# One decoder layer on one core: the score maxima of heads 2 to 4 moved ahead of the attention, and a higher rate for the recurrences

## The chip, the core and the metric

The kernel runs on one core of a Trainium2 chip. The metric is device time in microseconds (us) for one execution. TensorE (PE in the profile; its weight loads are PEld) does the matmuls, VectorE (DVE) the elementwise work and reductions, ScalarE (ACT) the activations and copies, GpSimd (POOL) some elementwise work; SyncE (SP), ACT and POOL issue the DMAs. Each engine takes its own instructions strictly in the order of the program, and semaphores tie them together. An instruction at the head of a queue that waits holds all that stands behind it on that engine.

## The reference

One layer of a hybrid decoder for 1024 prompt tokens and 8 single-token decode streams. One input projection of the residual is split among four head groups: a gated delta rule (A), RWKV-7 mixing (B), forgetting attention (C) and causal pooling (D). Each gives 512 columns, which are gated with a SiLU and go through one output projection and a layer norm. What the change touches is group C for the prompt, a causal attention of 8 heads of 64 with a decay in the scores:

```python
def _fox_block(qb, cqb, qpos, k, v, ck, kpos):
    s = jnp.einsum('nqhd,nshd->nhqs', qb, k) * (HEAD_DIM ** -0.5)
    s = s + jnp.swapaxes(cqb, 1, 2)[..., :, None] - jnp.swapaxes(ck, 1, 2)[..., None, :]
    s = jnp.where((kpos[None, :] <= qpos[:, None])[None, None], s, NEG_INF)
    return jnp.einsum('nhqs,nshd->nqhd', jax.nn.softmax(s, axis=-1), v)
```

The decode streams attend in the same way to 4096 cached tokens each, whose keys and values lie in pages in HBM.

## The kernel before, in words

The input projection comes as 57 column tiles of 128. A tile (`project`, line 343 on) is 144 matmuls: 16 slices of the depth, three groups of 344 token columns, and three products of split operands (lines 308 to 310). The last 24 tiles (`inputs_cd`) are the queries, the pooling inputs and gates, then keys, values and gates of group C.

Beside the tiles run *fillers*: Python generators that emit a piece of other work at each step. `fill` is called four times for each tile and adds a filler's rate to its account; the filler takes steps until the account is used up. In `inputs_cd` there are two: the cached attention's key side, and `recurrent` with the rate RATE_R. `recurrent` goes through the two recurrences (`chain_b`, `chain_a`), the pooling, the normalisation of group B, and last `c_first`, which starts on group C. What a generator has left when the tiles are done is emitted by `drain`, after the last tile. The emitted program is then put in an order by a scheduler, so that emission is a priority and not yet the order; but `anchored` ties what `c_first` issues to after the last projection matmul emitted so far (`self.last`).

The softmax of a head subtracts the exact row maximum. `c_max` makes it: for each of 8 blocks of 128 queries one or two matmuls of the queries and keys (tiles `cqm`, `ckx`, line 785, up to 512 columns), a mask (line 788), and a row maximum over them on DVE (tile `cmx`, line 789): 12 score tiles for a head. Then the 8 maxima are joined (`cm`, line 792), transposed on PE (line 794), negated by ACT (`cmt`, line 796) and split (`cmh`, `cml`). `c_scores` prepares a head: `c_load` brings queries and keys with four DMAs (`cqr`, `ckr`; lines 763 to 766) and copies them on ACT (`cqm` line 767, `ckx` line 769); the head's operands `cqq` (ACT, line 823), `cqx` (DVE, line 824) and `ckk` (POOL, lines 825 and 826) follow, then the maxima, which two small DMAs bring into the rows `cmr` (line 831) and DVE into `cqx` (line 832). `cqr` and `ckr` have one buffer each for all heads, so that the next head's `ckr` load waits until POOL has read this head's.

A head listed in EARLY has its maxima made ahead: `c_first` loads it, makes the maxima and keeps `cmh` and `cml`. Its `c_scores` later loads queries and keys once more, but leaves out the maxima. All the early heads share one `cqm` and one `ckx` buffer with head 0. Their score tiles (name `a`) have two PSUM buffers.

Then `branch_c` does the attention, head by head, 12 score tiles `s` for each, with `c_scores` of the head after next as a filler at rate 1.1 and the value side of the cached attention (`decode_v`, tile `dkv`) at 0.7. `c_attend` for a score tile: two matmuls (`s`, lines 849 and 850) and a mask, exp on ACT (`cpt`), a rounding copy on ACT (`cph`), a subtraction on DVE (`cpl`, line 861), and three value matmuls (`v`, lines 868 to 870). At the end of each half of a head DVE copies the numerator (`cnum`, line 873). The output projection (`o`) follows.

Of the kernel before, what the change touches and what calls it, by code (L numbers as in the profile page):

```python
# [17 lines left out]
N = T + NS  # L18
G3 = 344
GROUPS = (392, 384, 256)  # L20
RATE_R = 1.0
EARLY = (1,)
RATE_P = 1
SPOOL = {0: 99, 1: 99, 2: 0}
NPOOL = {392: 8, 384: 10, 256: 8}
# [154 lines left out]
class Kernel:  # L180
# [591 lines left out]
    def c_max(self, KX, QM, keep=""):  # L772

        nc = self.nc
        one = self.cp[0]
        mx = self.t(one, [128, 8, 2], "cmx", bufs=2)
        nc.gpsimd.memset(mx, NEG)
        for qi in range(8):
            for b in range((qi + 4) // 4):
                k0, k1 = 512 * b, min(512 * b + 512, 128 * qi + 128)  # L780
                n = k1 - k0
                w = max(n, 256)
                ps = self.ps(self.ctag())
                last = k1 == 128 * qi + 128
                nc.tensor.matmul(ps[:, :w], lhsT=QM[:, qi * 128:qi * 128 + 128], rhs=KX[0:66, k0:k0 + w],
                                 start=True, stop=not last)
                if last:
                    nc.tensor.matmul(ps[:, n - 128:n], lhsT=self.identb, rhs=self.mq, start=False, stop=True)
                nc.vector.reduce_max(mx[:, qi, b:b + 1], ps[:, :n], axis=AX.X)
            yield 1  # L790
        m8 = self.t(one, [128, 8], "cm8", bufs=2)
        nc.vector.tensor_tensor(m8, mx[:, :, 0], mx[:, :, 1], op=ALU.max)
        ps = self.ps(self.ctag())
        nc.tensor.transpose(ps[0:8, 0:128], m8, self.ident)
        mt = self.t(one, [8, 128], "cmt", bufs=1)
        nc.scalar.activation(mt, ps[0:8, 0:128], AF.Copy, scale=-1.0)
        mh, ml = (self.t(one, [8, 128], f"{x}{keep}", F32R, bufs=1) for x in ("cmh", "cml"))
        nc.vector.tensor_copy(mh, mt)
        nc.vector.tensor_tensor(ml, mt, mh.bitcast(F32), op=ALU.subtract)
        return mh, ml  # L800

    def c_first(self, pool):

        for h in EARLY:
            _, _, KX, QM = self.c_load(h, pool)
# [1077 lines left out]
    def inputs_cd(self, sp):  # L1883
# [3 lines left out]
        self.add(self.cached(), RATE_L)  # L1887
        self.add(self.recurrent(**R), RATE_R)
        for t in self.seq[33:]:
# [77 lines left out]
```

## Time and profile before

| | |
|---|---|
| median of 3 timed runs | 2399.89 us (2399.39 to 2400.68) |
| the profiled execution | 2396.94 us, of which the span of instructions is 2395.2 us |
| busy: PE, PEld, DVE, ACT, POOL | 2282.6, 2023.0, 1364.7, 938.4, 295.0 us |
| mean granted TensorE clock | 0.979 of full speed |
| last projection matmul starts | 1717.16 us after the span's start |
| attention of the 8 heads | 1717.3 to 1920.6 us |

A PE that is busy in the profile is not PE at its peak, since the ends of its pipelined matmuls are modelled. The stretch that matters here is the border between the last projection tile and the first heads of the attention; the rows of it stand below.

### The profile page before, as it was taken

To read this page: it belongs to the slowest core of one execution; us is meant where nothing else is said; L and a number is where in the kernel's file an instruction comes from. 1 tells how busy PE (TensorE), PEld (TensorE's weight loads), DVE (VectorE), ACT (ScalarE), POOL (GpSimd) and SP (SyncE) were. 2 spreads that over 40 slices of the span, in tenths; PEclk is the share of its full clock that TensorE was granted. 3 is DMA by queue.
4 is the path that set the end of the run, shared out by engine and by line. 5 is a ranking of instruction groups with operands and counts; after the bars stand their busy time and mean duration, and the time that the engine had idled before them with its cause. 6 is when DMAs were issued, how large, how long until landed. Compare 5 with 4: busy or idle time off the path is not lost. (4 is left out here: it accounts for less than half of the span.)

```text
span 2395.2 us, 47251 instructions
## 1 busy us (share of the span) xinstructions
PE 2282.6 (95%) x17640; PEld 2023.0 (84%) x17640; DVE 1364.7 (57%) x2676; ACT 938.4 (39%) x1853; POOL 295.0 (12%) x408
## 2 busy tenths in 40 slices
PE   8999999999899999999999999999899999999984
PEld 8999999998899999787787877899755578889984
DVE  4665757677576557432222245555578644564598
ACT  5644445434454444121111122454366665211244
POOL 0000000000000000103111121100132110100175
PEclk9999999999999999999999999999999999999997
DMA  6133323545523336778878888653488775683212
GB/s 215 56 100 95 104 85 95 151 106 120 113 81 94 89 107 142 172 187 264 274 250 283 259 273 288 232 161 107 124 260 248 223 282 192 219 304 129 88 63 88
DMA packets 369664, 402.44 MB, mean 168 GB/s; under 512 B 204877, under 2 KB 228350, under 8 KB 368666
## 3 DMA queue, kind: packets, MB, share of 16 engines
q1 hardware_dynamic: 307698, 263.83, 37.3%
q10 hardware_dynamic: 50056, 101.60, 13.9%
q0 software_dynamic: 11680, 33.99, 4.3%
q8 instruction: 139, 2.28, 0.4%
q14 instruction: 91, 0.75, 0.1%
HBM read 314.56 MB, written 84.67 MB: 167 GB/s over the span
## 5 line engine op out<-in xcount | busy, mean ns | idle before, releaser
L308 PE MATMUL pj<-xh,wlo 128*128 128x344 f32 x2688 | 873.1, 326 | 16.7 <-DVE wlo L303 8.6
L309 PE MATMUL pj<-xl,whi 128*128 128x344 f32 x2688 | 871.5, 324 | 0.0
L310 PE MATMUL pj<-xh,whi 128*128 128x344 f32 x2688 | 865.2, 324 | 0.0
L308 PEld LDWEIGHTS pj<-xh,wlo 128*128 128x128 f32 x2688 | 508.1, 189 | 37.1 <-issue 11.4
L309 PEld LDWEIGHTS pj<-xl,whi 128*128 128x128 f32 x2688 | 508.5, 189 | 19.8 <-issue 14.4
L310 PEld LDWEIGHTS pj<-xh,whi 128*128 128x128 f32 x2688 | 507.9, 189 | 16.4 <-issue 13.1
L302 ACT CAST whi<-raw 128x256 fp32r<-128x256 f32 (+1 forms) x504 | 213.0, 424 | 732.6 <-PE pj L310 530.2
L303 DVE TENSOR_TENSOR wlo<-raw,whi 128x256 fp32r<-128x256 f32 (+1 forms) x504 | 226.8, 452 | 365.5 <-ACT whi L302 356.1
L309 PE MATMUL o<-gl,whi 128*128 128x344 f32 x576 | 185.8, 323 | 0.0
L308 PE MATMUL o<-gh,wlo 128*128 128x344 f32 x576 | 184.6, 325 | 0.8 <-ACT gh L1695 0.5
L310 PE MATMUL o<-gh,whi 128*128 128x344 f32 x576 | 185.1, 321 | 0.0
L308 PEld LDWEIGHTS o<-gh,wlo 128*128 128x128 f32 x576 | 107.9, 188 | 21.8 <-DVE y L1720 9.4
L309 PEld LDWEIGHTS o<-gl,whi 128*128 128x128 f32 x576 | 109.0, 189 | 2.3 <-DVE ps L1221 0.9
L310 PEld LDWEIGHTS o<-gh,whi 128*128 128x128 f32 x576 | 109.0, 189 | 0.8 <-issue 0.8
L365 ACT ACTIVATE stg<-pj 128x344 f32<-128x344 f32 x168 | 74.6, 457 | 74.2 <-PE pj L310 73.0
L997 PE MATMUL k<-dkv,dqb 128*32 128x256 f32 x1024 | 88.4, 394 | 15.1 <-DMA dkv<-in_ck 9.0
L1720 DVE TENSOR_TENSOR y<-y,o 128x344 f32<-128x344 f32 x96 | 48.0, 510 | 57.3 <-PE o L310 57.0
L1105 PE MATMUL k<-dkv,dpT 128*8 128x512 f32 x512 | 71.5, 635 | 0.8 <-DMA dkv<-in_cv 0.8
L861 DVE TENSOR_TENSOR cpl<-cpt,cph 128x512 fp32r<-128x512 f32 (+1 forms) x96 | 60.9, 653 | 15.7 <-ACT cph L860 14.9
L308 PE MATMUL o<-gh,wkl 128*128 128x392 f32 (+2 forms) x192 | 63.9, 333 | 0.6 <-DVE wkl L303 0.5
L310 PE MATMUL o<-gh,wkh 128*128 128x392 f32 (+2 forms) x192 | 63.6, 331 | 0.0
L309 PE MATMUL o<-gl,wkh 128*128 128x392 f32 (+2 forms) x192 | 63.3, 330 | 0.0
(597 smaller groups left out, 3321.9 us busy)
## 6 DMA issues: line engine op xcount, KB each, us to landing
dkv<-in_ck SPq DMA_DIRECT2D x256, 256.0 KB
dkv<-in_cv SPq DMA_DIRECT2D x256, 256.0 KB
raw<-in_w ACTq DMA_DIRECT2D x228, 256.0 KB
out_pj<-stg ACTq DMA_DIRECT2D x33, 516.0 KB
bop<-bop SPq DMA_DIRECT2D x16, 1024.0 KB
raw<-in_wo ACTq DMA_DIRECT2D x64, 256.0 KB
aop<-aop SPq DMA_DIRECT2D x16, 768.0 KB
aop<-aost SPq DMA_DIRECT2D x40, 256.0 KB
```

What stands on the lines that cost most here:

```text
L302: nc.scalar.copy(hi, raw)
L303: nc.vector.tensor_tensor(lo, raw, hi.bitcast(F32), op=ALU.subtract)
L308: nc.tensor.matmul(ps, lhsT=wlo, rhs=xh, start=start, stop=False)
L309: nc.tensor.matmul(ps, lhsT=whi, rhs=xl, start=False, stop=False)
L310: self.last = nc.tensor.matmul(ps, lhsT=whi, rhs=xh, start=False, stop=stop).ins
L365: self.nc.scalar.activation(dst[:, g * G3:g * G3 + G3], ps[g], func)
L861: nc.vector.tensor_tensor(pl[:, off:], pt[:, off:], ph[:, off:].bitcast(F32), op=ALU.subtract)
L997: nc.tensor.matmul(ps[32 * hp:32 * hp + 32], lhsT=qb[:, hp, b], rhs=kt[:, :, hp], start=b == 0, stop=b == 7)
L1105: mm = lambda i: nc.tensor.matmul(po[32 * i:32 * i + 8], lhsT=pTv[:, c, :, 4 * bg + i], rhs=t[i // 2][:, i % 2], start=False, stop=c == 31)
L1720: nc.vector.tensor_tensor(y[:, s], y[:, s], ps[g], op=ALU.add)
```

## The change

The list EARLY goes from head 1 to heads 1 to 4, RATE_R from 1.0 to 1.3, and `c_max` gives way to the other fillers after every second block of queries instead of after each.

```diff
-RATE_R = 1.0
-EARLY = (1,)
+RATE_R = 1.3
+EARLY = 1, 2, 3, 4
...
                 nc.vector.reduce_max(mx[:, qi, b:b + 1], ps[:, :n], axis=AX.X)
-            yield 1
+            if qi % 2:
+                yield 1
```

In the order of instructions nothing changes on any engine for the first 7948 rows of PE, with both recurrences in them. From there on the normalisation of group B (tile names `py`, `pz`) and all of group C stand otherwise. One line more in the file moves line numbers above 789 up by one.

The first place is PE where the projection ends. Before, the matmul after the last projection tile (`pj`) is the first score tile of head 0's attention (`s`); the maxima of heads 1 and 0 stand earlier, among the projection's matmuls:

```order
L308 MATMUL pj_20934<-xh_28_130,wlo_21042 128x344
L309 MATMUL pj_20934<-xl_44_146,whi_21041 128x344
L310 MATMUL pj_20934<-xh_28_130,whi_21041 128x344
L849 MATMUL s_21174<-cqq_20424,ckk_20423 128x512
L850 MATMUL s_21174<-cqx_20425,ckx_20414 128x512
```

Now the maxima of heads 1, 2 and 3 stand among the projection's matmuls, and behind the last of these come head 3's transposed maxima (`cm_2727`) and then the score tiles `a` of head 4 (`ckx_20381`):

```order
L309 MATMUL pj_21151<-xl_44_146,whi_21242 128x344
L310 MATMUL pj_21151<-xh_28_130,whi_21242 128x344
L795 MATMUL a_20371<-cst_211,cm_2727_20369 8x128
L785 MATMUL a_20392<-ckx_20381,cqm_20382 128x256
L788 LDWEIGHTS identb_19595
L788 MATMUL a_20392<-mq_19597,identb_19595 128x128
L785 MATMUL a_20396<-ckx_20381,cqm_20382 128x256
```

After head 4's 12 tiles come the transposes of head 0's values and head 0's own 12 tiles (`ckx_20722`); here are the last of them and the first of the attention:

```order
L785 MATMUL a_20976<-ckx_20722,cqm_20723 128x512
L785 MATMUL a_20979<-ckx_20722,cqm_20723 128x512
L788 LDWEIGHTS identb_19595
L788 MATMUL a_20979<-mq_19597,identb_19595 128x128
L795 MATMUL a_21031<-cst_211,cm_2843_21029 8x128
L850 MATMUL s_21375<-cqq_20732,ckk_20731 128x512
L850 MATMUL s_21540<-cqq_20732,ckk_20731 128x384
L851 MATMUL s_21375<-cqx_20733,ckx_20722 128x512
```

What moved: 61 rows of PE (the maxima of heads 4 and 0 and 8 transposes) now stand between the last `pj` and the first `s`, with no other matmul among them.

The second place is ACT. Before, head 0's `cmt` stands among the copies of the projection's weights (`whi`), ahead of the evacuation of the last tile (`stg`) and of head 1's copies:

```order
L302 CAST whi_21019<-raw_20939 128x256
L381 DMA out_pj<-stg_20913 128x1032
L796 ACTIVATE cmt_20985<-a_20983 8x128
L302 CAST whi_21041<-raw_20939 128x256
L831 DMA cmr_19785<-cmh_2694_20290 1x4x128
L831 DMA cmr_19785<-cml_2695_20291 1x4x128
L365 ACTIVATE stg_21117<-pj_20932 128x344
L365 ACTIVATE stg_21117<-pj_20933 128x344
L365 ACTIVATE stg_21117<-pj_20934 128x344
L767 CAST cqm_21151<-cqr_21149 64x1024
```

Now it stands behind the loads and copies of heads 1 (names ending in 21349 to 21361) and 2 (21592 to 21604) and the load of head 3 (21944 and 21945); the last of these, with the first exp of the attention behind `cmt`:

```order
L767 CAST cqm_21595<-cqr_21593 64x1024
L824 CAST cqq_21604<-cqr_21593 128x1024
L765 DMA ckr_21592<-out_pj 64x1024
L766 DMA ckr_21592<-crow 4x1024
L763 DMA cqr_21945<-out_pj 64x1024
L769 CAST ckx_21594<-ckr_21592 68x1024
L764 DMA cqr_21945<-out_pj 64x1024
L765 DMA ckr_21944<-out_pj 64x1024
L766 DMA ckr_21944<-crow 4x1024
L767 CAST cqm_21947<-cqr_21945 64x1024
L797 ACTIVATE cmt_21033<-a_21031 8x128
L860 ACTIVATE cpt_21379<-s_21375 128x512
```

What moved: the score preparations of heads 1 and 2 come ahead of the first exp of head 0. The maxima of heads 2 to 4, which before stand among the score tiles of heads 0 to 3, are gone from there; those of heads 5 to 7 stand among the score tiles of heads 3 to 5, much as before.

## Rows read from the trace of the kernel before

**Rows 1.** Stretches: start:end us, busy us (instructions) of PE, PEld, DVE, ACT, POOL, PEclk, DMA share, GB/s.

```profile
1628.00:1717.40 89.40, 88.22 (x563) 85.43 (x562) 43.99 (x81) 30.45 (x56) 6.41 (x10) 1.00 0.29 81
1717.40:1757.40 40.00, 31.36 (x152) 16.87 (x151) 30.44 (x51) 26.64 (x48) 10.99 (x6) 0.79 0.87 259
1757.40:1807.50 50.10, 46.31 (x274) 27.31 (x274) 44.80 (x75) 34.17 (x68) 16.42 (x12) 1.00 0.90 265
1807.50:1874.90 67.40, 63.21 (x369) 38.97 (x368) 56.03 (x104) 44.66 (x91) 13.79 (x10) 0.97 0.79 239
1874.90:1920.60 45.70, 40.54 (x207) 22.85 (x206) 24.50 (x41) 26.45 (x53) 7.91 (x8) 0.89 0.77 240
1883.00:1889.00 6.00, 5.52 (x17) 2.69 (x18) 2.82 (x5) 2.77 (x6) 1.28 (x3) 0.50 0.63 208
```

**Rows 2.** Timeline of PE at the border: start us, us, engine, line, op, out<-in, shape.

```profile
1717.16 0.32 PE L310 MATMUL pj<-xh,whi 128*128 128x344 f32 x1
1717.32 0.39 PE L849 MATMUL s<-cqq,ckk 128*128 128x512 f32 x1
```

**Rows 3.** Timeline of DVE: the copies that end heads 0, 2, 4 and 5.

```profile
1756.74 0.68 DVE L873 COPY cnum<-v 64x512 f32<-64x512 f32 x1
...
1806.80 0.67 DVE L873 COPY cnum<-v 64x512 f32<-64x512 f32 x1
...
1856.32 0.67 DVE L873 COPY cnum<-v 64x512 f32<-64x512 f32 x1
...
1874.25 0.69 DVE L873 COPY cnum<-v 64x512 f32<-64x512 f32 x1 [1.15 <-PE v L870]
```

**Rows 4.** Groups of DVE, 1628 to 1717.3 us: busy us, mean ns | idle before, releasers.

```profile
L789 DVE TENSOR_REDUCE cmx<-a 128x1 f32<-128x512 f32 (+3 forms) x24 | 13.3, 557 | 14.8 <-PE a L785 7.8 <-PE a L788 6.9
...
L1229 DVE TENSOR_TENSOR stg<-stg,stg 128x1032 f32<-128x1032 f32 x3 | 3.7, 1234 | 1.5 <-ACT stg L1225 1.5
...
L768 DVE CAST cqm<-onec 2x1024 fp32r<-2x1024 f32 x4 | 2.7, 684 | 3.6 <-PE pj L310 2.7 <-PE a L785 0.8
```

**Rows 5.** Lines 824, 825 and 769 by themselves: duration ns min/median/max, first and last start.

```profile
L824 DVE TENSOR_TENSOR cqx<-cqr,cqm x8: 1206/1213/3372, 1660.9 to 1850.1; 64x1024 fp32r<-64x1024 f32 x8
...
L825 POOL TENSOR_TENSOR ckk<-ckr,ckx x8: 2367/2744/3080, 1661.6 to 1850.5; 64x1024 fp32r<-64x1024 f32 x8
...
L769 ACT CAST ckx<-ckr x9: 1032/1042/1053, 1633.2 to 1849.4; 68x1024 fp32r<-68x1024 f32 x9
```

**Rows 6.** Timeline of SP and ACT: two loads of queries, each with the copy that waits.

```profile
1633.85 0.60 SPq L764 DMA_DIRECT2D cqr<-out_pj  x1
...
1637.97 1.05 ACT L823 CAST cqq<-cqr 128x1024 fp32r<-128x1024 f32 x1 [2.79 <-DMA cqr<-out_pj]
...
1726.51 0.53 ACTq L764 DMA_DIRECT2D cqr<-out_pj  x1
...
1731.79 1.05 ACT L767 CAST cqm<-cqr 64x1024 fp32r<-64x1024 f32 x1 [1.09 <-DMA cqr<-out_pj]
```

**Rows 7.** Timeline of ACT and DVE: from head 0's transposed maxima to its operand.

```profile
1704.18 0.27 ACT L796 ACTIVATE cmt<-a 8x128 f32<-8x128 f32 x1 [0.48 <-DVE wlo L303]
...
1707.29 0.42 DVE L832 CAST cqx<-cmr 4x512 fp32r<-4x512 f32 x1 [0.20 <-DMA cmr<-cml]
```

**Rows 8.** Timeline of PE: a score tile with its mask among projection matmuls.

```profile
1640.93 0.48 PE L785 MATMUL a<-ckx,cqm 66*128 66x512 f32 x1
1641.25 0.23 PE L788 MATMUL a<-mq,identb 128*128 128x128 bf16 x1
1641.29 0.40 PE L308 MATMUL pj<-xh,wlo 128*128 128x344 f32 x1
```

**Rows 9.** Timeline: PE's longest gap in head 6.

```profile
1883.48 0.58 PE L870 MATMUL v<-cpl,cvh 128*128 128x256 f32 x1 [4.45 <-DVE cpl L861]
```

**Rows 10.** Timeline of POOL and DVE: a subtraction on each in head 0.

```profile
1719.99 2.92 POOL L825 TENSOR_TENSOR ckk<-ckr,ckx 64x1024 fp32r<-64x1024 f32 x1 [3.23 <-issue]
...
1720.61 3.37 DVE L824 TENSOR_TENSOR cqx<-cqr,cqm 64x1024 fp32r<-64x1024 f32 x1
```

## The prediction

> **What bounds the kernel now.** I read the busy time by stretches first [rows 1]. The last projection tiles are bound by PE: busy 88.2 of 89.4 us at full clock, with DVE and ACT at half or less. Behind them nothing is late: the last projection matmul starts at 1717.16 and the first score tile of the attention at 1717.32 [rows 2]. So the reader sees that the maxima of heads 1 and 0, which lie in that stretch, cost only their matmuls. The attention is another matter. DVE's copies at the ends of heads give the borders [rows 3]: head 0 takes 40.0 us, heads 1 and 2 together 50.1, heads 3 to 5 together 67.4, heads 6 and 7 together 45.7. In heads 1 and 2 DVE is busy 44.8 of 50.1 us; in heads 6 and 7, which have no maxima and no preparation beside them, 24.5 of 45.7. Head 0 is slow for another reason: PE is busy 31.4 of 40 us at a mean clock of 0.79, while ACT, POOL and the DMAs bring in heads 1 and 2. So there is something to gain in heads 0 to 2, and the order says what it is paid with.
>
> **The change part by part.** *The rate.* The first 7948 rows of PE are the same, with both recurrences in them: the higher rate emits the recurrences' steps earlier, and the order does not move them. What it moves is the normalisation of group B and, by some 26 rows of PE, the start on the early heads. Those stand beside a saturated PE; I cost this at nothing. If that cover failed, it would be a DMA that the projection waits for, and the matmul stream shows none in [rows 1].
>
> *One more head beside the projection.* Three heads' maxima stand there instead of two. A score tile with its mask takes 0.36 us from its start to the next projection matmul [rows 8]. Twelve of these are 4.3 us at most; eight of the twelve have a mask and half are narrower than 512 columns, so I take 3.2. The transposes of head 0's values go out of the stretch, and I take 0.7 off: **+2.5 us** (0 to 4.3).
>
> *The exposed stretch.* Heads 4 and 0 did not fit: between the last projection matmul and the first score tile of the attention PE now has 61 rows and nothing else to do. This is where I put the main cost, in two pieces.
>
> Up to head 4's last score tile, DVE sets the pace. Half of the 24 reductions are 6.65 us, the last tile's SiLU on DVE is three rows of 1.23, so 3.7, and two copies into `cqm` are 1.4 [rows 4]. The small rows about cancel with the overlap of one row's end with the next one's start: 11.7 us.
>
> From there ACT sets it, because head 0's `cmt`, without which no exp can be right, stands behind the preparations of heads 1 and 2, and each `ckr` load has to wait until POOL has read the one before. In order: two copies for head 0, 2.1 (1.04 each [rows 5]); POOL's subtraction, 2.7 [rows 5]; the two issues of the `ckr` load, of which one is ahead of the landing, 0.5, and the landing, 4.1 from the issue to the copy (1633.85 to 1637.97 [rows 6]); the copy, 1.0. That is 10.4. Then head 2's queries: 4.6 again, and two copies, 2.1, gives 17.1. Its keys: 4.6 and a copy, 1.0, gives 22.7. POOL's subtraction for head 2, 2.7, two issues for head 3, 1.0, its first copy, 1.0: 27.4. From the start of `cmt` to the end of the first copy from `cmr` it takes 3.5 us (1704.18 to 1707.71 [rows 7]): 30.9. Head 0's own 12 reductions run beside this and hide. Together **42.6 us** that had no counterpart: before, the same preparations ran beside head 0's attention.
>
> The bounds of this term: if ACT's chain hid wholly, DVE alone would be left, 13.3 for 24 reductions, 3.7, five copies into `cqm` 3.4, three subtractions into `cqx` 3.6, the two copies on ACT between head 4 and head 0, 2.1, and the 3.5 at the end: 29.6. If each of the three landings took as long as the other one in [rows 6] (1726.51 to 1731.79, 5.3, with page loads in the way), 46.2. The nearer row for a landing is the first, since the pages' five buffers fill early in the stretch and then nothing else runs; I keep 42.6.
>
> The Trainium skill has a price for a landing as well ("DMA: Bandwidth & Descriptors", section "Anatomy of one DMA"): about 2 us fixed and the bytes at 436 GB/s, which for 256 KB I estimate at 2.6 us. By it the three landings would be 4.5 us shorter and the sum 4.5 us lower; the two rows here are 4.1 and 5.3, and the rows stand.
>
> *Heads 0 to 2.* They lose three heads' maxima, and the preparations of heads 1 and 2. What is a head like then? Head 5 ran 17.9 us (1856.32 to 1874.25 [rows 3]). Heads 6 and 7 took 45.7, of which 4.45 is one wait [rows 9], so 20.6 each. The mean of the three is 19.7, and three heads are **59.1 us** in place of 40.0 + 50.1 = 90.1. Bounds: 17.9 and 22.9 (45.7 / 2) each, 53.7 to 68.6. Head 0 will start with PE's clock at the lower level, as behind the wait in head 6 (0.50 from 1883 to 1889 [rows 1]); that is up to 3 us, and I keep it for the range.
>
> *The rest.* The three early heads more load their keys and queries twice; the early loads stand beside the projection, where the DMAs are busy 0.29. On SP the loads of heads 2, 3, 4 and 0 now stand ahead of the page loads of the value side; head 0's waits for head 4's copies, which come a few us ahead of the last projection matmul, and the pages go into the space of the projection's operands, so they start behind that matmul before and after. Heads 3 to 7 keep their maxima and preparations, and the output projection comes behind unchanged: nothing.
>
> The sum: 2.5 + 42.6 + 59.1 - 90.1 = **+14.1 us**. The profiled execution took 2396.94 us (a span of 2395.2), so it would take 2411. It lies 3 us under the median of the runs, 2399.89; on that, which is what a time is compared with, I predict **2414 us**.
>
> **The rivals.** *ACT's chain hides and the heads run at PE's pace (faster).* The place is the same stretch. It decides from the point where the exposed stretch and three heads together stay under 87.6 us (90.1 less 2.5). For it: in heads 3 to 5 PE is busy 63.2 of 67.4 us [rows 1] with the 36 score tiles of three heads' maxima, 13 us by 0.36 each, so that without them a head could go down to some 17 us or less. Against it: heads 6 and 7 have nothing beside them and still took over 20. With 32 for the stretch and 16 for a head it gives 2.5 + 32 + 48 - 90.1 = -7.6, so 2392 us.
>
> *Cost and gain cancel (same).* A stretch of 34 us and heads of 18 give 2.5 + 34 + 54 - 90.1 = +0.4: 2400 us.
>
> *POOL and DVE hold each other up.* In head 0 DVE's subtraction took 3.37 us beside POOL's of 2.92 [rows 10], against a median of 1.21 [rows 5]. The stretch now has three such pairs, for heads 0, 1 and 2. If each meets, it is 3 x 2.2 = 6.5 us more: 2420 us. For it: both wait for the same copies on ACT. Against it: the median of DVE's eight is 1.21, so that most of them did not meet. The rule behind it is in the Trainium skill ("SBUF — State Buffer", section "Who interferes with whom"): a DVE instruction with two SBUF inputs and a GpSimd one that reads SBUF exclude each other for a whole instruction, while reductions are never held. Rows 10 agree.
>
> *The page loads take the place of DVE.* The DMAs are busy 0.90 in heads 1 and 2 [rows 1]. The pages of the value side are tied to the heads, and while PE is idle only five buffers' worth can come. If the pages then hold heads 0 to 2 to the pace of heads 1 and 2 (25.05 each, 75.2 together), the sum is +30: 2430 us. Against it: the other loads of that stretch have gone ahead, and the pages of three heads need no more bytes than before.
>
> That the change does not do what it says is certain in part and is in the sum: two of the five heads' maxima are beside no projection tile.
>
> **How the numbers follow.** 0.55 for the forecast (its own range 2405 to 2422), 0.12 for POOL and DVE, 0.10 for the pages, 0.13 for cancelling, 0.10 for faster. A measurement of this kernel can tell 0.2%, 4.8 us, from no change, so: slower 0.77, same 0.13, faster 0.10. The range for 8 in 10 leaves out the faster case and most of the pages': 2397 to 2428.
>
> **What would show it.** The last projection matmul at 1719 to 1720 us; between it and the first `s` about 40 us in which PE is busy less than half and 24 reductions run; `cmt` of head 0 late on ACT behind waits for `cqr` and `ckr`; head 2's end at about 1821 instead of 1807.5; heads 0 to 2 with DVE busy some two thirds of the time; the stretch from there to the end as long as before. I am wrong if the first exp comes within 30 us of the last projection matmul, or if heads 0 to 2 take over 25 us or under 16 each.

## The result, and the profile after

The changed kernel takes 2424.35 us (2420.48 to 2427.03, 4 runs) against 2399.64 us of the kernel before on the same chip: a ratio of 1.0102, with a 95% interval of 1.008 to 1.0124. It is slower by some 25 us. The forecast was 2414 us with a range of 2397 to 2428; the measured time lies inside it, and 2 us above the 2405 to 2422 that the forecast gave for its main case. The profiled execution after took 2420.48 us, its span is 2418.7 us, 23.5 more than before.

The stretches of the profile after come first; they answer to [rows 1] and have the same columns (start:end, busy us and instructions of PE, PEld, DVE, ACT and POOL, PEclk, DMA share, GB/s). Their borders are the last projection matmul, the first score matmul with head 0's maxima, the ends of heads 2 and 5, and the first and last matmul of the output projection.

```profile
1628.00:1712.70 84.70, 84.70 (x539) 80.92 (x537) 42.07 (x79) 29.94 (x51) 2.63 (x6) 1.00 0.27 76
1712.70:1757.00 44.30, 17.77 (x55) 10.35 (x53) 30.14 (x51) 16.01 (x22) 12.03 (x9) 0.56 0.58 180
1757.00:1829.80 72.80, 66.19 (x361) 39.48 (x361) 47.87 (x79) 49.03 (x99) 16.53 (x10) 0.94 0.78 230
1829.80:1897.60 67.80, 62.98 (x368) 38.60 (x367) 53.86 (x95) 45.41 (x91) 13.27 (x9) 0.97 0.82 242
1897.60:1948.60 51.00, 41.43 (x226) 21.68 (x224) 31.56 (x48) 34.77 (x66) 13.71 (x11) 0.93 0.82 268
1948.60:2392.80 444.20, 425.99 (x2674) 389.42 (x2674) 273.06 (x434) 149.40 (x272) 94.74 (x99) 0.98 0.51 170
```

The last two of these stretches in the kernel before, with the same borders:

```profile
1874.90:1920.40 45.50, 40.34 (x207) 22.65 (x205) 24.30 (x41) 26.45 (x53) 7.71 (x8) 0.89 0.76 239
1920.40:2369.50 449.10, 428.55 (x2694) 388.65 (x2694) 279.33 (x442) 156.75 (x285) 101.01 (x103) 0.98 0.51 174
```

The reader is to see three things. Between the projection and head 0 there is now a stretch of 44.3 us in which PE is busy 17.8 us and its granted clock is 0.56. Heads 0 to 2 behind it take 72.8 us instead of the 90.1 of [rows 1]. And the rest comes out even: heads 3 to 5 take 67.8 us instead of 67.4, and from the end of head 5 to the last matmul of the output projection it is 51.0 + 444.2 = 495.2 us instead of 45.5 + 449.1 = 494.6. Inside that sum heads 6 and 7 got faster (35.5 us) and the output projection began 15.5 us behind them, but what PE did there (the end of branch A and page matmuls) stands behind the output projection's start in the kernel before; nothing was won or lost by it. The projection ended 4.8 us earlier, at 1712.7 instead of 1717.5 us.

So the difference is -4.8 + 44.3 + 72.8 - 90.1 + 0.4 + 0.6 = +23.2 of the 23.5 us. By PE's own account, from the last projection matmul to the last one of the output projection, it was busy 614.4 us after and 609.8 before, and idle 65.7 after and 42.3 before. Of the 28.0 us by which this part grew, 23.4 are idle time of PE; in the new stretch alone it stands idle for 26.5 us.

These rows answer to [rows 2, 3]: the first score matmuls, and DVE's copies that end heads 2, 5 and 7 (start us, us, engine, line, op, out<-in; in brackets the idle time of the engine and what ended it).

```profile
1712.42 0.31 PE L310 MATMUL pj<-xh,whi 128*128 128x344 f32 x1
...
1752.82 1.09 PE L850 MATMUL s<-cqq,ckk 128*128 128x512 f32 x2
1757.00 0.80 PE L851 MATMUL s<-cqx,ckx 68*128 68x512 f32 x1 [3.08 <-DVE cqx L833]
...
1829.10 0.67 DVE L874 COPY cnum<-v 64x512 f32<-64x512 f32 x1
...
1896.95 0.69 DVE L874 COPY cnum<-v 64x512 f32<-64x512 f32 x1 [2.29 <-PE v L871]
...
1932.40 0.69 DVE L874 COPY cnum<-v 64x512 f32<-64x512 f32 x1 [0.20 <-PE v L871]
```

What PE waited for in the stretch from 1712.7 to 1757 us (engine, line, what it waited for: us in total, times, longest):

```profile
PE a L785 <- DVE cmx L789: 9.9, 9, 2.7
PE a L795 <- DVE cm L793: 7.1, 2, 5.1
PE a L745 <- ACT cqq L824: 3.7, 1, 3.7
PE s L851 <- DVE cqx L833: 3.1, 1, 3.1
PE a L785 <- ACT cmt L797: 2.6, 1, 2.6
```

These pieces follow one another. Head 4's score tiles run to 1729.0 us, the join of its maxima ends at 1732.5, the transposes of head 0's values take to 1738.2, head 0's tiles to 1752.5, and the way from the joined maxima to the operand `cqx` ends at 1757.0. The 9.9 us are score tiles that wait until DVE has read one of the two PSUM buffers.

### The profile page after: what moved, and what is told of

Its sections match the earlier page's. It is cut to its first block, busy times and chain, and to the rows that moved or that the text cites. A ratio compares the mean times of both kernels' runs of the same rounds, so it can differ in the third digit from the quotient of the medians.

```text
span 2418.7 us, 47306 instructions
## 1 busy us (share of the span) xinstructions
PE 2285.4 (94%) x17640; PEld 2024.6 (84%) x17640; DVE 1366.2 (56%) x2679; ACT 947.5 (39%) x1859; POOL 292.3 (12%) x408
## 4 chain that ended last, share of the span: by engine, by line
PE 78%; DMA 10%; DVE 5%; SPq 3%; issue 2%; ACT 1%; POOL 0%; ACTq 0%; DVEq 0%; POOLq 0%
PE pj L308 16%; PE pj L309 15%; PE pj L310 15%; PE o L308 5%; PE o L309 4%; PE o L310 4%; DMA dkv<-in_ck 3%; PE k L998 3%; PE k L1106 2%; DVE y L1752 1%; DVE y L1751 1%; DMA dkv<-in_cv 1%; DMA bop<-bop 1%; PE a L613 1%; PE a L463 1%
## 5 line engine op out<-in xcount | busy, mean ns | idle before, releaser
L308 PEld LDWEIGHTS pj<-xh,wlo 128*128 128x128 f32 x2688 | 506.3, 189 | 33.8 <-issue 11.6
L309 PEld LDWEIGHTS pj<-xl,whi 128*128 128x128 f32 x2688 | 506.5, 188 | 19.7 <-issue 14.4
L862 DVE TENSOR_TENSOR cpl<-cpt,cph 128x512 fp32r<-128x512 f32 (+1 forms) x96 | 67.9, 731 | 26.4 <-ACT cph L861 25.8
```

The costliest lines, as they stand in the source:

```text
L308: nc.tensor.matmul(ps, lhsT=wlo, rhs=xh, start=start, stop=False)
L309: nc.tensor.matmul(ps, lhsT=whi, rhs=xl, start=False, stop=False)
L862: nc.vector.tensor_tensor(pl[:, off:], pt[:, off:], ph[:, off:].bitcast(F32), op=ALU.subtract)
```

## The experiments

A caution first. PE's order up to the last projection matmul is the same in the changed kernel and in the runs e3 to e7, yet that matmul ended at 1712.7, 1718.4, 1712.1, 1726.7, 1723.8 and 1719.3 us. What makes this spread was not found. So traces are compared from that matmul on, and it stands beside the ratios of the timed runs. "Stretch" is from there to the first score matmul with head 0's maxima, "heads 0-2" from there to the end of head 2, "rest" from the last projection matmul to the end of the span.

| run | ratio to the kernel before (95%) | stretch | heads 0-2 | rest |
|---|---|---|---|---|
| before | 1 | 0 | 90.1 | 677.7 |
| after | 1.0102 (1.008 to 1.0124) | 44.3 | 72.8 | 706.0 |
| e1 rate only | 0.9995 (0.997 to 1.0021) | 0 | 91.1 | 680.8 |
| e2 heads 1, 2 | 1.0078 (1.0047 to 1.011) | 20.6 | 87.4 | 697.2 |
| e3 heads 1 to 3 | 1.0113 (1.0075 to 1.0151) | 33.2 | 75.5 | 702.6 |
| e4 ostg by POOL | 1.0104 (1.0073 to 1.0135) | 44.0 | 74.4 | 710.4 |
| e5 copies held back | 1.0158 (1.0128 to 1.0188) | 43.0 | 82.6 | 720.1 |
| e6 pages in the stretch | 1.018 (1.0156 to 1.0204) | 61.5 | 73.0 | 727.5 |
| e7 after, few page loads | 1.0025 (1.0008 to 1.0042) | 45.0 | 67.8 | 688.2 |
| e8 before, few page loads | 0.991 (0.9888 to 0.9933) | 0 | 90.5 | 660.8 |
| e9 e2 and copies held back | 1.0107 (1.0068 to 1.0145) | 19.6 | 94.9 | 703.4 |
| e10 short maxima | 1.0015 (0.9993 to 1.0037) | 14.8 | 77.4 | 685.6 |
| e11 values ahead | 1.0133 (1.0093 to 1.0173) | 45.2 | 71.0 | 703.2 |
| e12 before, short reductions | 1.0076 (1.0055 to 1.0096) | 0 | 96.6 | 697.4 |

**The change in parts.**

```diff
-EARLY = 1, 2, 3, 4
+EARLY = (1,)        # e1
+EARLY = 1, 2        # e2
+EARLY = 1, 2, 3     # e3
```

> The kernel before with the rate 1.3 and a pause only after every second block of queries; only head 1 is early. My step says that the rate by itself is worth nothing: PE's order keeps the maxima of heads 1 and 0 among the projection's matmuls and the first score tile directly behind the last of them. Expected 2400 us (2396 to 2404), last projection matmul at 1715 to 1719, no stretch behind it. The rival, that the earlier steps of the recurrences or the sparser pauses move time by themselves (by DMAs that collide with the projection's weights, or by maxima that end earlier in the late heads), expects more than 5 us in either direction, and heads 6 and 7 together at 36 to 40 us instead of 45.7.

Measured: no difference. The rate and the sparser pauses are worth nothing; the rival is out.

> The changed kernel with heads 1 and 2 early. Now the maxima of heads 1, 2 and 0 stand beside the projection and only 3 score matmuls and a transpose behind it. If the loss comes from the stretch in which PE has nothing but maxima, it is nearly gone: 6 to 10 us between the last projection matmul and the first usable score tile (the chain from the maxima to the operand is 3.5 to 4.3 of it), heads 0 to 2 at 78 to 84 us instead of 90.1, the page loads at most 5 us behind those of the kernel before, the first matmul of the output projection within 5 us of the last head: 2402 us (2394 to 2410). If instead the loss comes with every head whose maxima are ahead (its second load of keys and queries, the tiles among the projection's matmuls), it is a fourth to a third of the whole plus the chain: 2406 to 2412, with the last projection matmul at 1720 or later.

Measured: slower by 0.8%, and both theories missed. The stretch is 20.6 us although only 3 score matmuls are left in it, and heads 0 to 2 win 2.7 us, not 6 to 12. PE's waits behind the last projection matmul, then what POOL and DVE do there:

```profile
1726.76 0.38 PE L795 MATMUL a<-cst,cm 128*8 128x128 f32 x1 [9.05 <-DVE cm L793]
1726.86 1.09 PE L850 MATMUL s<-cqq,ckk 128*128 128x512 f32 x2
1737.72 0.80 PE L851 MATMUL s<-cqx,ckx 68*128 68x512 f32 x1 [9.78 <-DVE cqx L833]
```

```profile
1719.65 2.34 POOL L826 TENSOR_TENSOR ckk<-ckr,ckx 64x1024 fp32r<-64x1024 f32 x1 [3.78 <-issue]
1720.03 3.05 DVE L1222 SCALAR_TENSOR_TENSOR stg<-stg 128x1032 f32<-128x1032 f32 x1
1735.07 1.42 DVE L825 TENSOR_TENSOR cqx<-cqr,cqm 64x1024 fp32r<-64x1024 f32 x1 [4.73 <-ACT cqm L767]
1736.52 1.15 DVE L833 CAST cqx<-cmr 4x512 fp32r<-4x512 f32 x1
```

The end of head 0's maxima stands behind work of the last projection tile and of heads 0 and 1 on DVE, and head 0's operand (line 833) behind a subtraction (line 825) that waits for ACT. One head more that does not quite fit exposes the whole way from the maxima to the operand.

> The changed kernel with heads 1, 2 and 3 early, so that behind the last projection matmul only head 0's 12 score tiles and the transposes of its values are left, without head 4's 12 tiles. If the stretch is a row of pieces on DVE and PE, first head 4's tiles and then head 0's, it loses head 4's piece, 13 to 17 us: 24 to 28 us from the last projection matmul to the first score tile, head 2 gets head 4's maxima back (3 to 5 us), and the page loads come 10 to 15 us earlier than in the changed kernel: 2408 us (2403 to 2414). If ACT's chain (copies and loads of heads 1 and 2 ahead of head 0's transposed maxima) is what sets the end, as in my forecast, the stretch still has that chain whole, 31 to 34 us, and the time is 2413 to 2419.

Measured: 33.2 us of stretch and the time of the whole change. The stretch has the length that the theory of ACT's chain gave, but the waits say otherwise: 8.3 us are PE waiting for the load of head 0's values (`cvt`), 5.7 for `cqx`:

```profile
PE a L745 <- DMA cvt<-out_pj: 8.3, 1, 8.3
PE s L851 <- DVE cqx L833: 5.7, 1, 5.7
```

The time is above both expectations; I had counted on page loads that come earlier, and they bring nothing (e7).

**What sets the stretch.**

```diff
+        hold = self.cmt       # ACT's instruction that writes head 0's cmt
-        for _ in self.c_scores(1):
+        for _ in self.held(self.c_scores(1), hold):
...
-                g = self.c_scores(h + 2)
+                g = self.held(self.c_scores(h + 2), hold)
```

`held` runs each step of the generator so that what it puts on ACT is queued behind `hold`.

> The changed kernel, in which the loads and copies that ACT issues for heads 1 and later are queued behind head 0's cmt instead of ahead of it. If ACT's chain of loads and copies sets the end of the exposed stretch, as my forecast had it, the 44.3 us from the last projection matmul to the first score matmul with head 0's maxima (the row cqx,ckx of line 851 or its like) fall to 30 to 34, and head 0 gets a few us of the copies back: 2412 to 2418 us. The rival is that the stretch is set by the score tiles themselves, which wait for DVE with two PSUM buffers, and by the value transposes between the two heads: then it stays at 39 us or more and the time at 2420 to 2427.

Measured: the rival. ACT in the stretch of e5 (start us, us, engine, line, op, out<-in):

```profile
1752.98 0.37 ACT L749 CAST cvh<-a 128x256 fp32r<-128x256 f32 x1 [0.70 <-DVE cvl L750]
1763.81 0.27 ACT L797 ACTIVATE cmt<-a 8x128 f32<-8x128 f32 x1 [10.46 <-PE a L795]
1763.83 0.57 ACTq L763 DMA_DIRECT2D cqr<-out_pj  x1
```

ACT has nothing to do for 10.5 us ahead of head 0's `cmt`, no preparation of another head is in front of it, and yet the stretch is 43.0 us instead of 44.3. ACT's chain was long enough to explain the stretch, but the stretch hardly shortens without it.

Inside it something did move. The value transposes took 5.0 us instead of 5.7 and head 0's tiles 11.6 instead of 14.3, but the way from the joined maxima to the operand took 6.6 instead of 4.5, because DVE waited longer for the load of the maxima, beside which head 1's held-back loads now ran. This is DVE's copy (line 833) first in the changed kernel, then in e5:

```profile
1756.52 0.42 DVE L833 CAST cqx<-cmr 4x512 fp32r<-4x512 f32 x1 [2.35 <-DMA cmr<-cml]
1769.22 0.42 DVE L833 CAST cqx<-cmr 4x512 fp32r<-4x512 f32 x1 [4.58 <-DMA cmr<-cml]
```

So ACT's chain was worth some 3.5 us of the stretch at most, and 2.1 of these were lost again. The copies held back come due in head 0, which took 34.9 us from the operand on (29.3 in the changed kernel); the kernel is slower than the changed one.

> Heads 1 and 2 early, as in the second experiment, and ACT's loads and copies for the next heads queued behind head 0's cmt, as in the fifth. In the second, two waits of PE stand behind the last projection matmul, 9.1 us for the joined maxima (cm) and 9.8 us for the operand cqx, and ahead of the latter DVE waits for head 2's copies. Theory one, which the fifth experiment speaks for: the copies held back come due within head 0 and are lost there again, with what a later start of heads 1 and 2 costs: 2416 to 2432 us, with the wait for cqx at 4 to 6 us and head 0 at over 45. Theory two: where only the end of head 0's maxima is behind the projection, ACT's queue is what costs: 2403 to 2411 us.

Measured: theory one in the time. Head 0 took 34.6 us from the operand on, 48.6 from its first score matmul. The wait for `cqx` did not shrink, though: it is 13 us, since DVE's copy now stands behind the last tile's SiLU (line 1231), which waits 4.5 us for ACT:

```profile
1735.39 1.23 DVE L1231 TENSOR_TENSOR stg<-stg,stg 128x1032 f32<-128x1032 f32 x1 [4.47 <-ACT stg L1227]
1738.11 1.22 DVE L825 TENSOR_TENSOR cqx<-cqr,cqm 64x1024 fp32r<-64x1024 f32 x1 [1.49 <-ACT cqm L767]
1739.36 0.42 DVE L833 CAST cqx<-cmr 4x512 fp32r<-4x512 f32 x1
```

```diff
             self.early[h] = yield from self.c_max(KX, QM, h)
+            if h == 3:
+                while CV not in self.done:
+                    yield 1
+                yield from self.c_values(0)
```

(and `c_scores(0)` without them)

> The changed kernel with the transposes of head 0's values ahead of head 4's score tiles instead of between those and head 0's. The trace of the changed kernel cuts the 44.3 us behind the last projection matmul into head 4's tiles 16.3, the join of its maxima 3.5, the value transposes 5.7, head 0's tiles 14.3 and the way from the maxima to the operand 4.5. If these are a chain in which each waits for the one before, the transposes go into the time in which head 4's tiles wait for the transposed maxima of head 3 and for DVE, and the stretch falls to 38 to 41 us: 2418 to 2422 us. If ACT sets the end, which in that stretch copies for heads 0 to 2, the stretch stays at 43 us or more: 2422 to 2427.

Measured: 45.2 us, no shorter. PE now waits 7.3 us for the load of the values where head 4's tiles could run:

```profile
PE a L745 <- DMA cvt<-out_pj: 7.3, 1, 7.3
```

By its number this is the outcome given for ACT, but e5 showed ACT's chain to be worth only a few us; the wait has changed its place. No single link that was taken out (e5, e9, e11) made the stretch much shorter; the next one came up each time. Which links would have to go together was not settled.

**Can the stretch be filled?**

```diff
-        self.add(self.decode_v(vp), RATE_V[0])
+        dv = self.decode_v(vp)
+        for _ in range(9):
+            next(dv)
+        self.add(dv, RATE_V[0])
```

> The changed kernel, in which the first nine steps of the cached attention's value side (its set-up and the first eight groups of pages) are emitted ahead of the attention, so that they can run on PE between the score tiles of heads 4 and 0. If what is lost is PE's idle time in the stretch (26.5 us there against none before), the 8 to 10 us of PE work moved into it come off head 0: 2414 to 2419 us, with the stretch no longer than 47 us and head 0 at 24 to 28. If the time goes by when the pages start to flow, which would be some 30 us earlier, it falls further, to 2400 to 2410. If the page matmuls hold up the score tiles that stand behind them, the stretch grows by as much as head 0 loses: 2422 to 2430.

Measured: worse than the third outcome, and nothing came off heads 0 to 2, which took 73.0 us. The page matmuls stand between the score tiles, wait for pages themselves and run at the lower clock; a group of eight takes 1.90 us, against 1.05 in head 0 of the changed kernel. First that group in the changed kernel, from the timeline of PE:

```profile
1777.20 1.05 PE L1106 MATMUL k<-dkv,dpT 128*8 128x512 f32 x8
```

Then the stretch of e6 up to its first score matmul, with the columns of [rows 1], and two of its rows on PE:

```profile
1723.80:1778.90 55.10, 35.82 (x130) 11.98 (x129) 32.11 (x56) 15.80 (x21) 11.77 (x9) 0.55 0.93 267
```

```profile
1755.43 1.90 PE L1106 MATMUL k<-dkv,dpT 128*8 128x512 f32 x8 [2.99 <-DMA dkv<-in_cv]
1759.11 1.09 PE L745 MATMUL a<-cst,cvt 128*128 128x128 f32 x4 [1.77 <-ACT cqq L824]
```

**Are the pages late?** In the changed kernel no page load is issued between 1723 and 1769 us, and the loads of `ostg` for the output projection stand on SP behind page loads until 1941 us (1913.6 before). That made lateness of the pages the next suspect.

```diff
-            nc.sync.dma_start(r, self.G[4 * br + i])
+            (nc.gpsimd if br == 3 else nc.sync).dma_start(r, self.G[4 * br + i])   # e4
...
         def load(n):
+            if n >= bufs:                       # e7 (after), e8 (before)
+                tiles[n] = tiles[n - bufs]
+                return
```

> The changed kernel with the four loads of the first group's gated rows (tile ostg, line 1695) issued by POOL instead of SP, where they stand behind some 288 page loads. If the 15.5 us from the end of the last head to the first matmul of the output projection are owed to SP, whose page loads run some 20 us late because they stood still in the exposed stretch, that border shrinks to 2 to 5 us and the time goes to 2412 us (2409 to 2417). If it is owed to something else (the weights of the output projection, the end of branch A's recurrence on PE and ACT), the border stays at 13 us or more and the time at 2421 to 2427. A third way: the border shrinks but PE later waits for the late pages, so that 2418 to 2424 is left.

Measured: the border fell from 15.5 to 3.6 us, and the time stayed. The output projection then took 453.2 us instead of 444.2, since the work that stood ahead of it came behind, and heads 3 to 5 took 74.0. The third way is nearest, but without the wait for pages that it named (the whole attention has 6.2 us of them, 3.8 in the changed kernel).

> The changed kernel, which loads only the first five tiles of value pages and uses them again and again (it leaves out the other loads; all matmuls stay). It bounds what the transfers of the pages cost. If the loss of the change is PE's idle time and its order of work, this kernel stands above the kernel before with the same edit by 18 us or more. If it is pages that come late (SP's queue, the DMAs at 0.95 of their time in heads 1 and 2), the two without pages lie within 10 us of each other.

> The kernel before with the same edit: only five tiles of value pages are loaded. Expected 2380 to 2398 us, a few us below the kernel before, since PE waits for pages for less than 1 us in its attention and for nothing that SP brings in the output projection; heads 0 to 2 at 84 to 92 us. If the DMAs hold the attention of the kernel before back (their share is 0.87 to 0.90 in heads 0 to 2), it falls below 2380.

Measured: without the page loads both kernels get faster, the changed one by 0.8%, the one before by 0.9%, and the distance between them stays: 1.0025 / 0.991 = 1.0116, in the traces 688.2 - 660.8 = 27.4 us against 28.3. The transfers are not what the change costs. By its time, 2378 us, the kernel before falls just below the 2380 that stood for an attention held back by the DMAs, but its attention is hardly shorter, 200 us instead of 203. Heads 0 to 2 gain 5 us in the changed kernel and nothing in the one before; most of what both gain lies in the output projection (432.1 and 429.3 us instead of 444.2 and 449.1).

**Why heads 0 to 2 gained less than forecast.**

```diff
-            for b in range((qi + 4) // 4):
+            for b in range(1):                                      # e10, with EARLY = 1, 2, 3
                 k0, k1 = 512 * b, min(512 * b + 512, 128 * qi + 128)
+                if True:
+                    k0, k1 = max(0, 128 * qi - 128), 128 * qi + 128
...
-                nc.vector.reduce_max(mx[:, qi, b:b + 1], ps[:, :n], axis=AX.X)
+                nc.vector.reduce_max(mx[:, qi, b:b + 1], ps[:, n - 128:n], axis=AX.X)    # e12, on the kernel before
```

> Heads 1 to 3 early, and every head's maximum taken over its last 128 to 256 keys only (8 tiles of 256 columns instead of 12 of up to 512; the softmax is divided by its own sum, so what is subtracted only has to be near the maximum). With that the maxima of heads 1, 2, 3 and 0 are all beside the projection but for one transpose, and heads 0 and 1 have none beside them. It measures heads 0 and 1 without their maxima and without the stretch. My forecast's step says 19.7 us each, 39.4 together; the trace of the changed kernel says 33.4 and 20.4, so 50 to 54, because head 0 carries the set-up of the value side and PE there has no gap to give back. For the time: 2375 to 2385 us by the forecast's step, 2385 to 2400 by the other, of which 5 to 8 us come from the third of the tiles that is left out.

Measured: 30.1 and 19.0 us, 49.1 together, close to what the trace of the changed kernel said and 10 above my forecast's step. The stretch, head 0 from its operand on, and head 1:

```profile
1711.00:1725.80 14.80, 0.78 (x4) 0.20 (x3) 10.96 (x12) 7.41 (x9) 4.81 (x4) 0.58 0.97 315
1725.80:1755.90 30.10, 27.13 (x147) 15.70 (x151) 21.95 (x37) 20.93 (x42) 8.56 (x5) 0.92 0.75 226
1755.90:1774.90 19.00, 16.64 (x98) 9.96 (x96) 11.30 (x17) 14.30 (x27) 3.49 (x2) 1.00 0.92 245
```

Head 1 is the head that I had priced (19.7). Head 0 is not: PE is busy 27.1 us in it, with the set-up of the value side and the transposes of values beside its own tiles. The time is that of the kernel before, above both expectations: even with a third of the score tiles left out, what heads 0 and 1 gain about pays for the stretch of 14.8 us that three early heads still leave, and no more.

> The kernel before, in which every row maximum on DVE is taken over the last 128 columns of its score tile instead of all of up to 512 (the softmax is divided by its own sum, so what is subtracted only has to be near the maximum); PE's score tiles are the same. A reduction of 512 columns takes 0.69 us, one of 128 columns 0.29, so the 35 reductions of heads 0 to 2 give some 10 us of DVE back, and as much in heads 3 to 5. My forecast took heads 0 to 2 of the kernel before to be held by DVE, which is busy 75 of 90.1 us there: by that they shorten by 8 to 10 us and the time falls to 2382 to 2391. The other theory is that PE holds them: it is busy 77.7 of these 90.1 us, and what the maxima cost there is their 0.36 us each on PE: then heads 0 to 2 stay within 4 us of 90 and the time within 5 us of that of the kernel before.

Measured: DVE is busy 64.5 us in heads 0 to 2 instead of the 75.2 of [rows 1], and these heads take 96.6 us, not the 80 to 82 that DVE's pace would give. The stretch of heads 0 to 2:

```profile
1720.00:1816.70 96.70, 80.65 (x430) 46.88 (x428) 64.48 (x129) 60.94 (x115) 26.57 (x18) 0.86 0.90 251
```

Both theories missed the time. Less work on DVE did not shorten these heads, so the amount of its work is not what held them. It does not follow that PE alone does: with other durations the scheduler chose another order, in which PE waits longer for `cpl`. Over all eight heads it is this, first in the kernel before and then in e12:

```profile
PE v L870 <- DVE cpl L861: 5.5, 3, 4.4
PE v L870 <- DVE cpl L861: 14.7, 8, 6.0
```

In heads 0 to 2 alone these waits are 4.6 us instead of 0.6. Why that order is slower was not looked into.

None of the versions beats the kernel before.

## Why the prediction was right, and where it failed

- *The rate and the normalisation, nothing:* right (e1).
- *One more head beside the projection, +2.5:* measured -4.8, but this border differs by up to 14.6 us between kernels of the same order, so neither the term nor its sign can be read from the traces.
- *The exposed stretch, 42.6:* right in size, 44.3 us, and the trace shows what was to show it (24 reductions, PE under half busy). The size is partly luck. The first piece took 16.3 us instead of 11.7, the second 28.0 instead of 30.9, and the two errors nearly cancel. The second was also wrong in cause: 30.9 us were put on ACT's chain, and e5 took that chain away for 1.3 us. Two of the three landings that I priced at 4.1 us [rows 6] were faster: from the second issue to the copy they took 4.2 us (1734.64 to 1738.85), 3.1 (1740.13 to 1743.18) and 3.0 (1744.75 to 1747.78). The Trainium skill ("DMA: Bandwidth & Descriptors", section "Anatomy of one DMA", which is on GpSimd's path, while ACT issues these loads) gave an estimate of 2.6 us; two of the three lie nearer to it, and one to the row that I chose.
- *Heads 0 to 2, 59.1:* this is the step that failed. From the operand on they took 72.8 us, 13.7 more, and head 2 ended at 1829.8 instead of about 1821. Here are the three heads one by one, with the columns of [rows 1]:

```profile
1757.00:1786.30 29.30, 27.63 (x146) 15.68 (x150) 18.34 (x35) 18.20 (x38) 3.62 (x2) 0.90 0.54 172
1786.30:1806.70 20.40, 17.80 (x105) 10.99 (x97) 13.85 (x19) 14.41 (x28) 3.49 (x2) 1.00 0.90 248
1806.70:1829.80 23.10, 20.76 (x114) 12.82 (x114) 15.68 (x25) 16.41 (x33) 9.42 (x6) 0.93 0.99 286
```

  Head 1 came at about its price of 19.7 us. Head 0 took 9.6 us more, above the 25 that I had named as a sign of being wrong: PE is busy 27.6 us in it, 9.8 more than in head 1, with the set-up of the cached attention's value side and the transposes of two heads' values. Head 2 took 3.4 more, and six of head 5's score tiles already stand in it. The step took the pace of heads 5 to 7 for all three, because DVE, busy 44.8 of 50.1 us in heads 1 and 2, seemed to hold them. The same row has PE busy 46.3, and heads 0 to 2 together have 31.4 + 46.3 = 77.7 us of PE in 90.1. The 36 score tiles that went away are 36 x 0.36 = 13.0 of these [rows 8], so 64.7 stay, above the whole 59.1 that I gave. Measured are 66.2. That PE's work sets the pace there is read from these busy times; no run takes PE's work alone away. The sum with 72.8 in place of 59.1 and -4.8 in place of 2.5 is 42.6 + 72.8 - 4.8 - 90.1 = +20.5; the stretch adds 1.7, the rest 1.0. So it is partly luck that the time lies in the range: the border of the projection, 7.3 us better than forecast for a reason not found, hides half of this step's error.
- *The rest, nothing:* right as a sum (+1.0 us), though its border moved by 15 us.
- *The rivals.* ACT's chain did hide for the most part, but nothing was faster by that, and the heads' pace was the wrong part of that rival too. Cancelling failed on the same step. The pages, for which 2430 us was given, are excluded by e7 and e8, although heads 0 to 2 came near the pace that this rival gave them; without page loads they took 67.8 us, and head 0 still 29.4 (e7). POOL and DVE held each other up for long once, at the join of head 4's maxima: 2.30 us instead of 0.17.

```profile
1729.44 2.99 POOL L826 TENSOR_TENSOR ckk<-ckr,ckx 64x1024 fp32r<-64x1024 f32 x1 [17.06 <-ACT ckx L769]
1730.15 2.30 DVE L793 TENSOR_TENSOR cm<-cmx 128x8 f32<-128x8 f32 x1
...
1752.57 0.17 DVE L793 TENSOR_TENSOR cm<-cmx 128x8 f32<-128x8 f32 x1
```

That is 2.1 us and not 6.5, since DVE's three subtractions (line 825) took 1.22 us each. By the rule of the Trainium skill ("SBUF — State Buffer", section "Who interferes with whom") any DVE instruction with two SBUF inputs can be the one that is held. The trace agrees, and shows it for one that takes 0.17 us alone.

In short: PE is the engine that bounds the projection, and heads 0 to 2 of the kernel before have it busy 86% of the time. By the 0.36 us of a score tile, a maximum moved from the one to the other would cost there about what it saves here; no run measures that by itself. Two heads' maxima went into neither, but into a stretch of their own in which PE stands idle 26.5 us, and that idle time is the loss.

## What to carry to other kernels

Price a stage without some work by the busy time that is left on each of its engines, and take the largest as a floor, before taking the pace of a neighbour stage that looks alike; look above all for work that only the first piece of a stage has, as head 0 here. Work that is moved ahead of a stage must fit whole beside other work: the first piece that does not fit exposes the latency of the chain behind it, 20 us here for 3 score matmuls. A chain of waits that is as long as the gap is not yet its cause; take it away, and see whether the gap goes.

## What the runs showed of the hardware

- In the stretches of e2 to e6 and e9 to e11, in which PE kept falling idle, its granted clock was 0.53 to 0.58 on the mean, so work put into such a gap runs mostly at the lower of the two levels: 1.90 us for a group of eight page matmuls against 1.05.
- POOL's subtraction holds a DVE instruction of two inputs for its whole length: 3.37 us in e10 and 3.05 in e2, where 1.2 is usual; in e10 POOL's next instruction held a copy of 0.2 us as well. The rows are from e10:

```profile
1713.63 2.34 POOL L828 TENSOR_TENSOR ckk<-ckr,ckx 64x1024 fp32r<-64x1024 f32 x1 [2.08 <-issue]
1713.69 3.37 DVE L827 TENSOR_TENSOR cqx<-cqr,cqm 64x1024 fp32r<-64x1024 f32 x1
1716.04 1.91 POOL L829 CAST ckk<-ckx 64x1024 fp32r<-64x1024 f32 x1
1716.98 1.05 DVE L801 CAST cmh<-cmt 8x128 fp32r<-8x128 f32 x1
```

- The small load of a head's maxima landed later where other loads ran beside it. From the issue of its second part (line 832) to DVE's copy that waits for it (line 833) it took 1.7 us in the changed kernel, with the DMAs busy 0.01 of that time, 4.0 in e5 (busy 0.84) and 4.1 in e6 (0.76).
- The same order of instructions on PE ended the projection anywhere between 1712.1 and 1726.7 us. A few us of a single trace in a part that a change does not touch say nothing.
